# Low parts and gated products on VectorE, nine-step reciprocal roots, and ctx ahead of x in the last part of a SwiGLU layer

## The chip, the core and the metric

The kernel runs on one core of one Trainium2 chip (trn2). The metric is the device time of one execution in microseconds (us), the median of three runs. A core has TensorE (PE in the profile, its weight loads PEld), VectorE (DVE), ScalarE (ACT), GpSimd (POOL), SyncE (SP, which issues the weight DMAs here) and DMA engines.

## What is computed

Two transformer blocks of two layers each, width 1024, 512 tokens of x and, in the second block, 256 tokens of a context ctx. All in fp32. Cut to what matters here:

```
# first block, two layers
h = rms_norm(x, g_norm1[l]) * (1 + sc1) + sh1
u = h @ w_in[l] + b_in[l]                       # latents, stick-breaking q/k/v, gates
x = x + gt1 * (merged @ w_out[l])               # merged: two attentions, gated
h = rms_norm(x, g_norm2[l]) * (1 + sc2) + sh2
up = causal_depthwise_conv(h @ w_up[l], w_conv[l], b_conv[l])
a, v_ff = split(up)
x = x + gt2 * ((silu(a) * v_ff) @ w_down[l])    # silu(a) * v_ff: the gated product
# second block, layer 0: convolution mixer for x and ctx, then
x = x + gf_x * rmsnorm(swiglu(fx, w1, w3, w2), g)
ctx = ctx + gf_c * rmsnorm(swiglu(fc, w1, w3, w2), g)
# layer 1: attention, queries of x, keys and values of x and ctx; then swiglu of x alone
```

mod (sh, sc, gt) comes from products of a silu vector with modulation weights; the second block has one such vector for x and one for ctx.

## The kernel before, in words

Activations lie transposed, 8 tiles of 128 features by 512 tokens. A matmul in fp32 quality is made of three in a faster format: each weight chunk and each activation is split into a high part (rounded, `hi`) and a low part (`lo` = value minus high), and `dense` (L176 to L186) adds hi*hi, hi*lo and lo*hi in PSUM (L184, L185, L186). `dense_tok` (L188 to L194) does the same with the activation as the stationary side.

`weights` (L157 to L168) loads a chunk of 128 x up to 1024 by SP's DMA queue into `raw`, lets ACT round it into `whi` (L165), and subtracts to get `wlo` (L168). The subtraction runs on VectorE, or on POOL for each `lo_pool`-th chunk. `lo_pool` is 2 from the first full-width up of a first-block layer to that layer's end, 1 in the last part of the attention loop (`WO_LATE`), 2 for the output projection of the second half (`LO_O`), and 0 elsewhere. So half of the chunks of a first-block feed-forward stretch have their low part made by POOL.

That stretch (the last third of `first_layer`) has 22 pairs of ups in three parts, FFN_PARTS, with eight downs behind each part. `up` (L731 to L753) multiplies both branches, ACT and VectorE make the three-tap convolution from PSUM (L740, L744, L745), ACT makes Silu (L751), POOL the gated product (L752), and `split` makes the high part on ACT (L282) and the low part on VectorE (L285). A down's result is added to x by VectorE (L778), which also frees the PSUM tile. The first three pairs and the last downs run in two halves of 256 tokens. Between these, side work multiplies modulation weight rows by one vector (layer 0) or two (layer 1) on VectorE (L308, tiles `mjunk`), in program order.

`rstd_psum` (L226 to L244) sums squares by matmuls with a column of 1/1024 (L238), adds epsilon on VectorE (L240), calls `rsqrt` (L197 to L211), and broadcasts the root by transposes (L243). `rsqrt` starts from an integer shift and subtraction (L204, L205), halves (L206), and repeats three steps three times (L208 to L210). `modulate` and `post_norm` use the broadcast: of eight feature tiles VectorE takes five products (L261), POOL three (L259).

In the second block `ffn2` runs a list of steps by part; each step is an up or a down for a group of streams: sx is all of x, sa and sb its halves, st is ctx. At the last part's downs, `ffn_done` is called per stream: post norm and residual, then the pre norm for attention. In `attention_layer`, `PROJ` is the order of projections: (stream, g) with stream 0 = A, 1 = B (halves of x), 2 = ctx, and g = a half of the query heads or None for keys and values. Queries and keys are normed per head (with `rsqrt` again), turned by rope (VectorE L1082, POOL L1084) and transposed by TensorE (L1091). Then come 64 units of scores, with the output projection of the first half of x (w_o) inside the loop; that of the second half follows behind it.

The order within each engine's queue is fixed at build time by a planner that simulates the engines' times and takes instructions in program order where that is free; TensorE, VectorE, ACT and POOL then each run their queue in order, and waits are by semaphores between queues.

Of the kernel before, what the change touches and what calls it, by code (L numbers as in the profile page):

```python
# [81 lines left out]
LO_O = 2  # L82
# [14 lines left out]
class Core:  # L97


    def __init__(self, ctx, tc, a):  # L100
        self.tc, self.nc, self.a = tc, tc.nc, a
        nc = self.nc
        self.const = ctx.enter_context(tc.tile_pool(name="const", reuse_waits="tile", bufs=1))
        self.res = ctx.enter_context(tc.tile_pool(name="res", reuse_waits="tile", bufs=1))
        self.wp = ctx.enter_context(tc.tile_pool(name="wp", reuse_waits="tile", bufs=1))
        self.sm = ctx.enter_context(tc.tile_pool(name="sm", reuse_waits="tile", bufs=4))
        self.ps = None
        c = self.const
# [12 lines left out]
        self.chunks = 0  # L121
        self.lo_pool = 0
# [36 lines left out]
    def weights(self, src, n):  # L159
# [37 lines left out]
    def rsqrt(self, v, n, step=False):  # L197
        nc = self.nc
        y = self.sm.tile([P, 32], F32, tag="rs_y", name="rs_y", bufs=3)
        hv = self.sm.tile([P, 32], F32, tag="rs_h", name="rs_h", bufs=2)  # L200
        b = self.sm.tile([P, 32], F32, tag="rs_b", name="rs_b", bufs=2)
        y, hv, b = y[:, :n], hv[:, :n], b[:, :n]
        t = b.bitcast(I32)
# [21 lines left out]
    def rstd_psum(self, sums):  # L225
# [9 lines left out]
        v = self.sm.tile([P, 4], F32, tag="rs_v", name="rs_v", bufs=2)  # L235
# [4 lines left out]
        nc.vector.tensor_scalar(v[:, :nt], ps[:, :nt], EPS, None, op0=ALU.add)  # L240
        r, last = self.rsqrt(v[:, :nt], nt, True)
# [141 lines left out]
def mla_heads(core, tmp, pool, kp, l, ups, cos, sin, rows):  # L383
# [28 lines left out]
    for w, width in enumerate((256, 128)):  # L412
        nc.vector.tensor_scalar(vv[:, :, w], ss[:, :, w], 1.0 / width, EPS, op0=ALU.mult, op1=ALU.add)
# [56 lines left out]
    vq = sm.tile([P, 16], F32, tag="vq", name="vq", bufs=1)  # L470
    nc.vector.tensor_scalar(vq, ssq, 1.0 / 192, EPS, op0=ALU.mult, op1=ALU.add)
# [26 lines left out]
    vk = sm.tile([P, 16], F32, tag="vk", name="vk", bufs=1)  # L498
    nc.vector.tensor_scalar(vk, ssk.rearrange("p a b -> p (a b)"), 1.0 / 192, EPS, op0=ALU.mult, op1=ALU.add)
    rk = core.rsqrt(vk, 16)  # L500
# [166 lines left out]
def first_layer(core, pool, l, ups, mod, cos, sin, next_mod, early, finish):  # L667
# [58 lines left out]
    with tc.tile_pool(name=f"ff{l}", reuse_waits="tile", bufs=1) as fp:  # L726
        tails = {}

        def up(i, hl, cols):
# [22 lines left out]
            nc.gpsimd.tensor_tensor(av[0], av[0], av[1], op=ALU.mult)  # L752
            core.split(hl[0][:, cols], hl[1][:, cols], av[0])  # L753

        for part, (k0, k1) in enumerate(FFN_PARTS):
# [5 lines left out]
            if part == 0:  # L761
                next_mod(fp)
                core.lo_pool = 2
# [21 lines left out]
        core.lo_pool = 0  # L785
# [54 lines left out]
def ffn2(core, fp, i, bases, parts, nbuf, finish):  # L840
# [3 lines left out]
    for part, (k0, k1, steps) in enumerate(parts):  # L844
        first, last = part == 0, part == len(parts) - 1
        hid = {b.tag: [core.pair(fp, b.n, "hid" + b.tag, nbuf) for _ in range(k0, k1)] for b in bases}
        core.lo_pool = 0
# [35 lines left out]
    core.lo_pool = 0  # L883


def conv_layer(core, X, A, B, T, post, pre, between):
# [4 lines left out]
    with tc.tile_pool(name="cv_c", reuse_waits="tile", bufs=1, side="right") as cp, ExitStack() as es:  # L891
# [92 lines left out]
        core.lo_pool = CONV_LO  # L984
# [28 lines left out]
        core.lo_pool = 0  # L1013
# [29 lines left out]
def attention_layer(core, pool, A, B, T, axial, tables, dense_psum, finish):  # L1043
# [4 lines left out]
    with ExitStack() as es:  # L1048
# [8 lines left out]
        with tc.tile_pool(name="at_t", reuse_waits="tile", bufs=1) as tmp:  # L1057
# [39 lines left out]
            def keys(st, pss):  # L1097
# [5 lines left out]
                nc.vector.tensor_scalar(v, v, 1.0 / 64, EPS, op0=ALU.mult, op1=ALU.add)  # L1103
                rk = core.rsqrt(v, 8)
# [33 lines left out]
            core.lo_pool = PROJ_LO  # L1138
            for st, g in PROJ:
# [6 lines left out]
                if g == 1:  # L1146
                    v = rq[half].rearrange("p a b -> p (a b)")
                    nc.vector.tensor_scalar(v, v, 1.0 / 64, EPS, op0=ALU.mult, op1=ALU.add)
                    nc.vector.tensor_scalar(v, core.rsqrt(v, 32), float(64.0 ** -0.5), None, op0=ALU.mult)
            core.lo_pool = 0  # L1150
# [3 lines left out]
        with tc.tile_pool(name="at_p", reuse_waits="tile", bufs=1) as pp, core.psum_pool("ps_a") as pa:  # L1154
# [69 lines left out]
            for u in range(64 + 4):  # L1224
# [26 lines left out]
        core.lo_pool = 0  # L1251
# [3 lines left out]
def emit(tc, a, out, stop=None):  # L1255
    nc = tc.nc
    with ExitStack() as ctx:
# [147 lines left out]
        with tc.tile_pool(name="y0", reuse_waits="tile", bufs=1) as yp:  # L1405
# [12 lines left out]
            def ffn_done(s):  # L1418
# [9 lines left out]
                     (18, 22, [(up, [sx]), (down, [sa]), (down, [sb]), (up, [st]), (down, [st])]))  # L1428
# [144 lines left out]
```

## Time and profile before

| what | us |
|---|---|
| median of three runs (3200.9, 3206.35, 3206.95) | 3206.35 |
| the profiled execution's own time | 3205.2 |
| its span, first to last instruction | 3203.2 |
| TensorE busy | 3026.3 |
| VectorE busy | 2094.5 |
| ScalarE busy | 1378.0 |
| GpSimd busy | 556.8 |
| mean granted TensorE clock | 0.976 |

A group's row of the profile reads: line, engine, operation, output<-inputs by the program's names, shapes, xcount, then busy us, mean ns of one, and idle time of the engine just before them with what ended it. A timeline's row reads: start, duration, engine, line, operation, and in brackets the wait before it and who ended it. Matmuls are pipelined and their ends modelled.

### The profile page before, as it was taken

How to read it: one execution, taken by the hardware profiler on the slowest of the kernel's cores; microseconds unless marked ns; L12 is line 12 of the kernel's file. 1: busy time of each engine (PE TensorE's matmuls, PEld its weight loads, DVE VectorE, ACT ScalarE, POOL GpSimd, SP SyncE). 2: the span in 40 equal slices, each digit the busy share in tenths (PEclk: the TensorE clock that was granted, in tenths of full speed). 3: DMA queues.
4: the chain of work that ended last, by engine and by line, in shares of the span. 5: the costliest groups of instructions: out<-in, count | busy, mean ns of one | idle time of the engine just before them, and what ended most of it. 6: DMA issues, size and time to landing. Idle time of an engine off the chain costs nothing.

```text
span 3203.2 us, 45064 instructions
## 1 busy us (share of the span) xinstructions
PE 3026.3 (94%) x16916; PEld 2541.2 (79%) x16916; DVE 2094.5 (65%) x3973; ACT 1378.0 (43%) x2521; POOL 556.8 (17%) x508
## 2 busy tenths in 40 slices
PE   6999999999899999999999899999999889999998
PEld 5776888888777697777866688888888667898887
DVE  7654785657643588798898686544549976673336
ACT  4534562335534563224522574221226556553223
POOL 4000223333000213223334120000002311210001
PEclk9999999999999999999999899999999889999999
DMA  6443346554321254554544345234435310243323
GB/s 235 135 147 100 120 164 204 176 203 143 100 66 56 85 193 154 180 193 138 160 140 123 106 145 178 87 118 135 134 101 167 121 35 17 76 144 109 98 98 120
DMA packets 129322, 416.69 MB, mean 130 GB/s; under 512 B 16208, under 2 KB 21840, under 8 KB 129104
## 3 DMA queue, kind: packets, MB, share of 16 engines
q1 hardware_dynamic: 123984, 404.96, 38.8%
q0 software_dynamic: 2048, 4.43, 0.5%
q10 hardware_dynamic: 3072, 4.43, 0.5%
q8 instruction: 133, 2.18, 0.3%
q14 instruction: 85, 0.70, 0.1%
HBM read 402.81 MB, written 2.10 MB: 126 GB/s over the span
## 4 chain that ended last, share of the span: by engine, by line
PE 42%; DVE 7%; ACT 1%; DMA 1%; issue 1%; POOL 0%; ACTq 0%; DVEq 0%; POOLq 0%
PE pa L185 4%; PE pa L184 4%; PE pa L186 4%; PE pv L186 3%; PE pv L184 3%; PE pv L185 3%; PE dn L186 3%; PE dn L184 3%; PE dn L185 3%; PE cv L948 2%; PE yps L1198 2%; DVE wlo L168 1%; DVE hp L261 1%; PE pT L1187 1%; PE sc L1165 1%
## 5 line engine op out<-in xcount | busy, mean ns | idle before, releaser
L165 ACT CAST whi<-raw 128x1024 fp32r<-128x1024 f32 (+4 forms) x622 | 599.3, 967 | 1008.4 <-PE dn L185 296.4
L168 DVE TENSOR_TENSOR wlo<-raw,whi 128x1024 fp32r<-128x1024 f32 (+4 forms) x543 | 620.9, 1145 | 366.0 <-ACT whi L165 357.6
L184 PE MATMUL dn<-hi,whi 128*128 128x256 f32 (+1 forms) x1088 | 361.9, 336 | 19.4 <-DVE x L778 13.5
L185 PE MATMUL dn<-lo,whi 128*128 128x256 f32 (+1 forms) x1088 | 362.6, 335 | 1.6 <-DVE lo L285 1.5
L186 PE MATMUL dn<-hi,wlo 128*128 128x256 f32 (+1 forms) x1088 | 359.7, 334 | 3.3 <-DVE wlo L168 3.1
L184 PE MATMUL up<-hh,whi 128*128 128x512 f32 (+1 forms) x800 | 292.0, 366 | 7.2 <-ACT hh L269 7.2
L185 PE MATMUL up<-hl,whi 128*128 128x512 f32 (+1 forms) x800 | 292.6, 366 | 0.4 <-DVE hl L270 0.4
L186 PE MATMUL up<-hh,wlo 128*128 128x512 f32 (+1 forms) x800 | 291.8, 365 | 0.0
L259 POOL TENSOR_TENSOR hp<-hp,rb 128x256 f32<-128x256 f32 x90 | 76.5, 862 | 1151.0 <-ACT hp L258 1136.6
L168 POOL TENSOR_TENSOR wlo<-raw,whi 128x1024 fp32r<-128x1024 f32 (+1 forms) x79 | 194.1, 2458 | 391.9 <-ACT whi L165 388.7
L308 DVE SCALAR_TENSOR_TENSOR mjunk<-mraw,crow 128x1024 f32<-128x1024 f32 (+1 forms) x176 | 220.5, 1253 | 42.9 <-PE g L185 21.1
L184 PEld LDWEIGHTS dn<-hi,whi 128*128 128x128 f32 x1088 | 205.8, 190 | 47.0 <-issue 14.0
L186 PEld LDWEIGHTS dn<-hi,wlo 128*128 128x128 f32 x1088 | 205.2, 189 | 28.2 <-DVE wlo L168 5.5
L185 PEld LDWEIGHTS dn<-lo,whi 128*128 128x128 f32 x1088 | 206.7, 190 | 25.0 <-DVE lo L285 2.3
L184 PE MATMUL pa<-hh,whi 128*128 128x512 f32 (+1 forms) x496 | 179.8, 362 | 7.1 <-ACT hh L269 6.4
L185 PE MATMUL pa<-hl,whi 128*128 128x512 f32 (+1 forms) x496 | 178.6, 360 | 0.2
L186 PE MATMUL pa<-hh,wlo 128*128 128x512 f32 (+1 forms) x496 | 178.0, 359 | 0.0
L184 PEld LDWEIGHTS up<-hh,whi 128*128 128x128 f32 x800 | 152.3, 191 | 31.6 <-ACT hh L269 7.7
L185 PEld LDWEIGHTS up<-hl,whi 128*128 128x128 f32 x800 | 152.6, 191 | 24.7 <-DVE hl L270 1.0
L186 PEld LDWEIGHTS up<-hh,wlo 128*128 128x128 f32 x800 | 152.4, 191 | 23.6
L860 DVE TENSOR_TENSOR s<-s,pv 128x512 f32<-128x512 f32 (+1 forms) x76 | 40.9, 539 | 196.0 <-PE pv L186 196.0
L186 PE MATMUL pv<-hh,wlo 128*128 128x512 f32 (+1 forms) x432 | 152.6, 353 | 0.7 <-DVE wlo L168 0.7
(471 smaller groups left out, 7349.5 us busy)
## 6 DMA issues: line engine op xcount, KB each, us to landing
raw<-in_w SPq DMA_DIRECT2D x148, 512.0 KB, 3.5
raw<-in_w_up SPq DMA_DIRECT2D x100, 512.0 KB, 3.5
mraw<-in_w_modt SPq DMA_DIRECT2D x96, 512.0 KB, 3.5
mraw<-in_w_adat SPq DMA_DIRECT2D x80, 512.0 KB, 3.4
raw<-in_w_pw SPq DMA_DIRECT2D x56, 512.0 KB, 3.4
raw<-in_w_down SPq DMA_DIRECT2D x48, 448.0 KB, 3.4
raw<-in_w_g SPq DMA_DIRECT2D x32, 512.0 KB, 3.2
raw<-in_w_out SPq DMA_DIRECT2D x32, 512.0 KB, 3.5
```

What stands on the lines that cost most here:

```text
L165: nc.scalar.copy(hi[:, :n], raw[:, :n])
L168: eng.tensor_tensor(lo[:, :n], raw[:, :n], hi[:, :n], op=ALU.subtract)
L184: mm(out, lhsT=hi[:, k, :], rhs=xh[:, cols], start=(k == 0), stop=False)
L185: mm(out, lhsT=hi[:, k, :], rhs=xl[:, cols], start=False, stop=False)
L186: mm(out, lhsT=lo[:, k, :], rhs=xh[:, cols], start=False, stop=(k == n - 1))
L259: nc.gpsimd.tensor_tensor(p, p, rb[1], op=ALU.mult)
L261: nc.vector.scalar_tensor_tensor(p, x, scale, rb[0], op0=ALU.mult, op1=ALU.mult)
L308: behind(nc.vector.scalar_tensor_tensor(junk, raw, 1.0, v, op0=ALU.mult, op1=ALU.mult, accum_out=d[:, f : f + 1]))
L860: nc.vector.tensor_tensor(s, s, pv, op=ALU.mult)
L948: nc.tensor.matmul(ps[32 * g : 32 * g + 32, :], lhsT=wt[:, 8 * g + j, :], rhs=ug[g][:, 4 * j : 4 * j + S], start=(j == 0), stop=(j == 7))
L1165: nc.tensor.matmul(ps[:, b, :384], lhsT=q, rhs=khT[:, hd // 4, ks], start=True, stop=False)
L1198: nc.tensor.matmul(yps[64 * e : 64 * e + 64, :], lhsT=V[j][:, kvh * 64 : (kvh + 1) * 64], rhs=pairs[p][1][e][:, j, :], start=(j == 0), sto ...
```

## The change

All low parts of weights are made on VectorE: `lo_pool`, `PROJ_LO`, `CONV_LO`, `WO_LATE` and `LO_O` go. The gated product of the first block goes from POOL to VectorE. `rsqrt` takes scale, epsilon and a factor in its first instruction and needs nine instructions, with a start and steps of other constants; the instructions that added epsilon and scaled around it go, and two that multiplied behind it become copies. In the last part of the first SwiGLU layer of the second block, up and down of ctx come first, then up of x and the downs of its halves; the keys and values of ctx become the first projection.

```diff
-PROJ = ((0, 0), (0, 1), (0, None), (1, 0), (1, None), (2, None), (1, 1))
-WO_LATE = 3
+PROJ = ((2, None), (0, 0), (0, 1), (0, None), (1, 0), (1, None), (1, 1))
...
         nc.scalar.copy(hi[:, :n], raw[:, :n])
-        self.chunks += 1
-        eng = nc.gpsimd if self.lo_pool and self.chunks % self.lo_pool == 0 else nc.vector
-        eng.tensor_tensor(lo[:, :n], raw[:, :n], hi[:, :n], op=ALU.subtract)
+        nc.vector.tensor_tensor(lo[:, :n], raw[:, :n], hi[:, :n], op=ALU.subtract)
...
-    def rsqrt(self, v, n, step=False):
+    def rsqrt(self, v, n, scale=1.0, factor=1.0, step=False):
...
-        nc.vector.tensor_scalar(t, v.bitcast(I32), 1, None, op0=ALU.logical_shift_right)
-        nc.vector.tensor_scalar(y.bitcast(I32), t, -1, 0x5F3759DF, op0=ALU.mult, op1=ALU.add)
-        nc.vector.tensor_scalar(hv, v, -0.5, None, op0=ALU.mult)
-        for _ in range(3):
-            nc.vector.tensor_tensor(b, y, y, op=ALU.mult)
-            nc.vector.tensor_tensor(b, b, hv, op=ALU.mult)
-            last = nc.vector.scalar_tensor_tensor(y, b, 1.5, y, op0=ALU.add, op1=ALU.mult)
+        k = -0.5 / (3.375 * factor) ** 2
+        nc.vector.tensor_scalar(w, v, scale * k, EPS * k, op0=ALU.mult, op1=ALU.add)
+        nc.vector.tensor_scalar(y.bitcast(I32), w.bitcast(I32), -0.5, float(0x5F375A86 - 2**22 - 2**30),
+                                op0=ALU.mult, op1=ALU.add)
+        nc.vector.tensor_tensor(b, y, y, op=ALU.mult)
+        nc.vector.tensor_tensor(b, b, w, op=ALU.mult)
+        nc.vector.scalar_tensor_tensor(c, b, 5.0 / 3.0, b, op0=ALU.add, op1=ALU.mult)
+        nc.vector.scalar_tensor_tensor(c, c, 1.25, y, op0=ALU.add, op1=ALU.mult)
+        nc.vector.tensor_tensor(b, c, c, op=ALU.mult)
+        nc.vector.tensor_tensor(b, b, w, op=ALU.mult)
+        last = nc.vector.scalar_tensor_tensor(y, b, 2.0 / 3.0, c, op0=ALU.add, op1=ALU.mult)
...
-        nc.vector.tensor_scalar(v[:, :nt], ps[:, :nt], EPS, None, op0=ALU.add)
-        r, last = self.rsqrt(v[:, :nt], nt, True)
+        r, last = self.rsqrt(ps[:, :nt], nt, step=True)
...
-    rq0 = core.rsqrt(vq, 16)
+    rq0 = core.rsqrt(ssq, 16, 1.0 / 192, 192.0 ** -0.5)
     rq = sm.tile([P, 16], F32, tag="rq", name="rq", bufs=1)
-    nc.vector.tensor_scalar(rq, rq0, float(192.0 ** -0.5), None, op0=ALU.mult)
+    nc.vector.tensor_copy(rq, rq0)
...
             nc.scalar.activation(av[0], av[0], AF.Silu)
-            nc.gpsimd.tensor_tensor(av[0], av[0], av[1], op=ALU.mult)
+            nc.vector.tensor_tensor(av[0], av[0], av[1], op=ALU.mult)
...
                 v = ss.rearrange("p a b -> p (a b)")
-                nc.vector.tensor_scalar(v, v, 1.0 / 64, EPS, op0=ALU.mult, op1=ALU.add)
-                rk = core.rsqrt(v, 8)
+                rk = core.rsqrt(v, 8, 1.0 / 64)
...
-                     (18, 22, [(up, [sx]), (down, [sa]), (down, [sb]), (up, [st]), (down, [st])]))
+                     (18, 22, [(up, [st]), (down, [st]), (up, [sx]), (down, [sa]), (down, [sb])]))
```

## Rows read from the trace of the kernel before

**Rows 1.** The page's first part: an engine's busy us, share, instructions.

```profile
PE 3026.3 (94%) x16916; PEld 2541.2 (79%) x16916; DVE 2094.5 (65%) x3973; ACT 1378.0 (43%) x2521; POOL 556.8 (17%) x508
```

**Rows 2.** Busy time by stretch, core 0: layer 0, then layer 1 of the first block.

```profile
core 0: us, PE busy (x) PEld busy (x) DVE busy (x) ACT busy (x) POOL busy (x), PEclk, DMA share, GB/s
485.00:755.00 270.00, 269.53 (x1208) 221.86 (x1206) 156.09 (x222) 92.64 (x117) 84.07 (x42) 1.00 0.55 180
...
1240.00:1500.00 260.00, 247.39 (x1062) 201.13 (x1061) 223.09 (x291) 83.49 (x105) 74.82 (x36) 0.97 0.55 178
```

**Rows 3.** TensorE's waits, whole span: total us, times, longest us.

```profile
PE rb L243 <- DVE rs_y L210: 19.8, 11, 4.1
PE dn L184 <- DVE x L778: 13.5, 5, 6.9
...
PE rb L238 <- DVE acc L221: 12.6, 3, 9.7
```

**Rows 4.** Busy time by stretch: the passage to attention, and just before it.

```profile
2393.00:2593.00 200.00, 167.40 (x971) 143.20 (x971) 182.29 (x436) 116.91 (x216) 63.22 (x65) 0.92 0.42 135
...
2350.00:2393.00 43.00, 43.00 (x205) 36.14 (x204) 13.36 (x16) 11.48 (x16) 0.00 (x0) 1.00 0.22 68
```

**Rows 5.** The page's fifth part: low parts on POOL (busy us, mean ns | idle).

```profile
L168 POOL TENSOR_TENSOR wlo<-raw,whi 128x1024 fp32r<-128x1024 f32 (+1 forms) x79 | 194.1, 2458 | 391.9 <-ACT whi L165 388.7
```

**Rows 6.** Groups of POOL, 1240 to 1500 us.

```profile
L168 POOL TENSOR_TENSOR wlo<-raw,whi 128x1024 fp32r<-128x1024 f32 x18 | 47.2, 2624 | 53.0 <-ACT whi L165 53.0
...
L752 POOL TENSOR_TENSOR up<-up 128x512 f32<-128x512 f32 x14 | 18.1, 1291 | 110.6 <-DVE up L745 92.5 <-ACT up L740 18.1
```

**Rows 7.** Timeline of VectorE, 1274 to 1285 us: start, us, line, operation.

```profile
1275.77 3.27 DVE L308 SCALAR_TENSOR_TENSOR mjunk<-mraw,ccrow 128x1024 f32<-128x1024 f32 x1
```

**Rows 8.** Timeline of POOL, the same stretch; two instructions in one row.

```profile
1274.66 6.58 POOL L168 TENSOR_TENSOR wlo<-raw,whi 128x1024 fp32r<-128x1024 f32 x2 [3.99 <-ACT whi L165]
```

**Rows 9.** Timeline of TensorE, the same stretch; in brackets the wait before.

```profile
1279.85 0.47 PE L184 MATMUL dn<-hi,whi 128*128 128x512 f32 x1 [3.09 <-DVE x L778]
```

**Rows 10.** Groups of VectorE, 1240 to 1500 us, with POOL at work.

```profile
L308 DVE SCALAR_TENSOR_TENSOR mjunk<-mraw,ccrow 128x1024 f32<-128x1024 f32 x46 | 63.4, 1379 | 0.7
L308 DVE SCALAR_TENSOR_TENSOR mjunk<-mraw,crow 128x1024 f32<-128x1024 f32 x45 | 59.8, 1328 | 3.0 <-DMA mraw<-in_w_modt 2.6
L285 DVE TENSOR_TENSOR lo<-up,hi 128x512 fp32r<-128x512 f32 x14 | 28.4, 2030 | 19.2 <-ACT hi L282 19.2
```

**Rows 11.** Groups of VectorE, 2000 to 2400 us, with POOL idle.

```profile
L308 DVE SCALAR_TENSOR_TENSOR mjunk<-mraw,crow 128x1024 f32<-128x1024 f32 x40 | 48.8, 1219 | 3.2 <-DMA mraw<-in_w_modt 3.2
...
L168 DVE TENSOR_TENSOR wlo<-raw,whi 128x1024 fp32r<-128x1024 f32 x33 | 40.4, 1224 | 32.7 <-ACT whi L165 32.4
...
L285 DVE TENSOR_TENSOR lo<-s,hi 128x512 fp32r<-128x512 f32 x18 | 12.4, 691 | 9.8 <-ACT hi L282 9.6
...
L308 DVE SCALAR_TENSOR_TENSOR mjunk<-mraw,ccrow 128x1024 f32<-128x1024 f32 x8 | 9.8, 1221 | 0.1
```

**Rows 12.** Timeline of VectorE: a root at the second half's output projection.

```profile
2778.47 0.16 DVE L240 TENSOR_SCALAR rs_v<-rb 128x2 f32<-128x2 f32 x1 [0.94 <-PE rb L238]
...
2780.25 2.25 DVE L208 TENSOR_TENSOR rs_b<-rs_y 128x2 f32<-128x2 f32 x1
```

**Rows 13.** Timeline of TensorE behind it: two waits.

```profile
2796.96 0.58 PE L186 MATMUL wo<-hh,wlo 128*128 128x256 f32 x1 [3.10 <-DVE wlo L168]
...
2811.03 0.58 PE L184 MATMUL pa<-hh,whi 128*128 128x256 f32 x1 [1.66 <-ACT hh L269]
```

**Rows 14.** Groups of VectorE in the passage to attention, 2393 to 2593 us.

```profile
L168 DVE TENSOR_TENSOR wlo<-raw,whi 128x1024 fp32r<-128x1024 f32 x39 | 50.2, 1288 | 4.6 <-ACT whi L165 4.5
...
L221 DVE TENSOR_TENSOR acc<-acc,sqx 128x256 f32<-128x256 f32 x36 | 17.4, 491 | 0.1
...
L168 DVE TENSOR_TENSOR wlo<-raw,whi 128x512 fp32r<-128x512 f32 x21 | 14.9, 721 | 2.5 <-ACT whi L165 2.4
...
L270 DVE SCALAR_TENSOR_TENSOR ctx_hl<-hp,mod,ctx_hl 128x256 fp32r<-128x256 f32 x8 | 4.4, 593 | 0.0
```

**Rows 15.** TensorE's waits in the same passage.

```profile
PE pj L192 <- DVE rp L1082: 4.8, 1, 4.8
```

More of the change, by code (lines that the diff above doesn't have):

```diff
@@ L81 @@
 YB = 1
-LO_O = 2
 GATE_TAGS = ("hp",) * 5 + ("rb",) * 3 + ("acc",) * 2 + ("sqx",) * 4
@@ L120, in __init__ @@
         self.side = iter(())
-        self.chunks = 0
-        self.lo_pool = 0
     def issue_behind(self, ins, others):
@@ L194, in dense_tok @@
         mm(out, lhsT=xl[:, cols], rhs=wh, start=False, stop=last)
-    def rsqrt(self, v, n, step=False):
+    def rsqrt(self, v, n, scale=1.0, factor=1.0, step=False):
         nc = self.nc
+        w = self.sm.tile([P, 32], F32, tag="rs_w", name="rs_w", bufs=2)
         y = self.sm.tile([P, 32], F32, tag="rs_y", name="rs_y", bufs=3)
-        hv = self.sm.tile([P, 32], F32, tag="rs_h", name="rs_h", bufs=2)
         b = self.sm.tile([P, 32], F32, tag="rs_b", name="rs_b", bufs=2)
-        y, hv, b = y[:, :n], hv[:, :n], b[:, :n]
-        t = b.bitcast(I32)
-        nc.vector.tensor_scalar(t, v.bitcast(I32), 1, None, op0=ALU.logical_shift_right)
-        nc.vector.tensor_scalar(y.bitcast(I32), t, -1, 0x5F3759DF, op0=ALU.mult, op1=ALU.add)
-        nc.vector.tensor_scalar(hv, v, -0.5, None, op0=ALU.mult)
-        for _ in range(3):
-            nc.vector.tensor_tensor(b, y, y, op=ALU.mult)
-            nc.vector.tensor_tensor(b, b, hv, op=ALU.mult)
-            last = nc.vector.scalar_tensor_tensor(y, b, 1.5, y, op0=ALU.add, op1=ALU.mult)
+        c = self.sm.tile([P, 32], F32, tag="rs_c", name="rs_c", bufs=2)
+        w, y, b, c = w[:, :n], y[:, :n], b[:, :n], c[:, :n]
+        k = -0.5 / (3.375 * factor) ** 2
[9 more added lines that the diff above has]
+        last = nc.vector.scalar_tensor_tensor(y, b, 2.0 / 3.0, c, op0=ALU.add, op1=ALU.mult)
         return (y, last) if step else y
@@ L234, in rstd_psum @@
             ps, pb = self.mm_psum("ms"), self.at_psum("rb")
-        v = self.sm.tile([P, 4], F32, tag="rs_v", name="rs_v", bufs=2)
         for t in range(nt):
@@ L412, in mla_heads @@
     for w, width in enumerate((256, 128)):
-        nc.vector.tensor_scalar(vv[:, :, w], ss[:, :, w], 1.0 / width, EPS, op0=ALU.mult, op1=ALU.add)
+        nc.vector.tensor_scalar(vv[:, :, w], ss[:, :, w], 1.0 / width, None, op0=ALU.mult)
     r = core.rsqrt(v, 8)
@@ L469, in mla_heads @@
         nc.vector.tensor_copy(qrT[:, :, sl], tp.rearrange("p (a b) -> p a b", b=P))
-    vq = sm.tile([P, 16], F32, tag="vq", name="vq", bufs=1)
-    nc.vector.tensor_scalar(vq, ssq, 1.0 / 192, EPS, op0=ALU.mult, op1=ALU.add)
-    rq0 = core.rsqrt(vq, 16)
+    rq0 = core.rsqrt(ssq, 16, 1.0 / 192, 192.0 ** -0.5)
     rq = sm.tile([P, 16], F32, tag="rq", name="rq", bufs=1)
-    nc.vector.tensor_scalar(rq, rq0, float(192.0 ** -0.5), None, op0=ALU.mult)
+    nc.vector.tensor_copy(rq, rq0)
     wkv = core.chunk(a["w_ukv"][l])
@@ L497, in mla_heads @@
         kt.append(kn)
-    vk = sm.tile([P, 16], F32, tag="vk", name="vk", bufs=1)
-    nc.vector.tensor_scalar(vk, ssk.rearrange("p a b -> p (a b)"), 1.0 / 192, EPS, op0=ALU.mult, op1=ALU.add)
-    rk = core.rsqrt(vk, 16)
+    rk = core.rsqrt(ssk.rearrange("p a b -> p (a b)"), 16, 1.0 / 192)
     for t in range(TOK):
@@ L762, in first_layer @@
                 next_mod(fp)
-                core.lo_pool = 2
             for i in range(k0 + apart, k1):
@@ L784, in first_layer @@
                     finish(cols, sums)
-        core.lo_pool = 0
 class Base:
@@ L882, in ffn2 @@
             yield
-    core.lo_pool = 0
 def conv_layer(core, X, A, B, T, post, pre, between):
@@ L983, in conv_layer @@
         us = []
-        core.lo_pool = CONV_LO
         core.side = taps_dve(us)
@@ L1012, in conv_layer @@
         es.close()
-        core.lo_pool = 0
         pre(T)
@@ L1136, in queries @@
                                qT[half][2 * g + hb][:, :, t * P : t * P + P], hb == 1)
-            core.lo_pool = PROJ_LO
             for st, g in PROJ:
@@ L1147, in attention_layer @@
                     v = rq[half].rearrange("p a b -> p (a b)")
-                    nc.vector.tensor_scalar(v, v, 1.0 / 64, EPS, op0=ALU.mult, op1=ALU.add)
-                    nc.vector.tensor_scalar(v, core.rsqrt(v, 32), float(64.0 ** -0.5), None, op0=ALU.mult)
-            core.lo_pool = 0
+                    nc.vector.tensor_copy(v, core.rsqrt(v, 32, 1.0 / 64, 64.0 ** -0.5))
         dense_psum.close()
@@ L1250, in attention_layer @@
             B.squares(core, B.yv(m), m)
-        core.lo_pool = 0
         finish(B)
```

6 lines of the change are left out of this document (removed).

## The prediction

> **What bounds the kernel now.** I read the page first, then the busy time by stretch, then TensorE's waits, then the stretches where it waits. TensorE is busy for 94% of the span [rows 1], so nothing off its path is worth anything where it is full, and the whole 177 us that it is idle is the most that better feeding could give. The up and down stretch of the first block's layer 0 shows a full stage: TensorE 269.53 of 270 us, VectorE 156 [rows 2]. The same stretch of layer 1 isn't full: TensorE 247 of 260 at a mean granted clock of 0.97, VectorE 223 [rows 2]. The difference is the side work: two modulation rows per weight row there, one in layer 0. TensorE's longest waits by cause are the broadcast that waits for a reciprocal root (19.8 us in 11 waits), down matmuls that wait until VectorE has emptied their PSUM (13.5), and sums that wait for VectorE's additions (12.6) [rows 3]. The worst long stretch is the passage from the second block's first SwiGLU layer to attention: in 200 us TensorE is busy for 167 at a clock of 0.92, while VectorE is busy for 182; just before it, in the last ups of x, TensorE is full and VectorE works 13 of 43 us [rows 4]. So there VectorE is the bound, and some of its work could be done earlier.
>
> **Low parts and gated product.** By the code, 35 low parts of each first-block layer and nine of the second block are on POOL: the 79 of the page [rows 5]. With them go 50 gated products, of 512 and 256 columns. POOL takes 2.6 us for a low part and 1.3 for a product [rows 6]; the question is what VectorE pays. Alone, VectorE takes about 1.22 us for 1024 elements from two SBUF tensors and 0.69 for 512 [rows 11]. So 22 low parts and 14 products of the stretch of layer 1 add 22 x 1.22 + 14 x 0.69 = 36 us to VectorE's 223 of 260. But it already pays for POOL's work: a modulation row that begins at 1275.77 takes 3.27 us [rows 7], and it ends 1.1 us, its own working time, after POOL's first low part (two of them fill 1274.66 to 1281.24, half of that is 3.29 [rows 8]). It stood still until POOL was done. Behind it stands the emptying of a PSUM tile, for which TensorE waits 3.09 us [rows 9]. Over this stretch the split's low part takes 2030 ns against 691 alone, the two kinds of modulation row 1379 and 1328 against 1221 and 1219 [rows 10, 11]: 14 x 1.34 + 46 x 0.16 + 45 x 0.11 = 31 us that go with POOL's work. Net, VectorE gets 5 us more in 260. That is within its 37 idle us, but in order, so it can help or hurt: bounds are minus 20 us (260 less 247 that TensorE is idle [rows 2], and some of the slow clock behind its waits) and plus 10 (the 5 us twice, with the clock lost behind). The product adds a wait to VectorE, for Silu on ACT, with the low parts and the emptying of PSUM queued behind it; Silu reads the first branch's tile, which is done while TensorE still multiplies the second (24 x 0.22 us), so the wait should be nothing. I take minus 3: the net is near nothing, and the chain up, Silu, product, hi, lo gets 0.6 us shorter at each pair (1.29 to 0.69), which counts at the layer's end.
> In layer 0 the same addition lies beside a full TensorE (156 plus some 36 of 270): 0; without that cover it would cost what exceeds VectorE's 114 idle us, which is nothing. The five low parts inside attention take at most 5 x 1.23 = 6 us if each stands in front of a maximum that TensorE needs; I take 0, since POOL's broadcast of the totals is freed of a predecessor of 2.5 us [rows 5] as well. At the output projection of the second half, a step of the root is held from 0.16 to 2.25 us by POOL [rows 12], and TensorE waits 3.10 us for a low part and 1.66 for the first h [rows 13]. Four low parts more cost 4 x 1.23 = 4.9 us on VectorE; three such holds give back 3 x 2.1 = 6.3. Bounds plus 5 and minus 5, taken: minus 2.
> A rule speaks against this: the Trainium skill (Perfetto Trace Analysis, Optimizing Scalar/DVE Operations) says that with VectorE saturated some work may be moved to ScalarE or even GpSimd; that would make this part a loss, which is the second rival. The same place warns that the two share an SBUF read port, so that this need not help, and with the warning the trace agrees [rows 7 to 11].
>
> **Shorter roots.** The code goes from 13 VectorE instructions a root (addition of epsilon, shift, subtraction, halving, three times three) to nine. Dependent steps are 0.18 us apart (2778.47 to 2780.25 is ten steps) [rows 12], so an exposed root gets 3 to 4 steps, some 0.6 us, shorter; halving lay beside another step. There are 31 roots of norms and 11 of heads and latents by the code. Exposed are those before which TensorE waits: the 11 waits of [rows 3] less three in the attention passage, counted below, plus the start and three or four hidden behind "sum" and h waits: 13 x 0.6 = 8 us. Lower bound 4 (only the eight seen), upper 14 (where a step stands behind other work in VectorE's queue, each step saved saves an instruction of 0.4 to 1.2 us, too). The multiplication after the roots of q becomes a copy of the same size: 0.
>
> **ctx ahead of x.** Up and down of ctx move before the ups of x, with their 8 + 8 weight DMAs, ACT's rounding and VectorE's low parts; keys of ctx become the first projection. SP's weight queue keeps its order of need, and no queue gets more to do. What moves off VectorE's crowded stretch: 8 low parts at 0.72 and 8 at 1.29 (16.1 us), a third of the 36 additions (5.9), ctx's own low halves (4.4) [rows 14], and, alike for ctx as for each half of x, its additions, products and splits (some 14, estimated from five to eight each at 0.4 to 0.55) and a third of the roots' steps (5): 45 us of 182. It goes under the ups of x, where VectorE is idle for 30 of 43 us [rows 4], and under its own 288 half-width matmuls. These, at half of 0.223 us (270 us by 1208 matmuls [rows 2]), are 32 us of TensorE, 35 with the two sums. So 165 of the 200 us stay, with 137 us of VectorE work, 129 with shorter roots (8 off: 12 roots by four steps of 0.16 us). At its present share (182 of 200) that is 142: minus 23. Not all of it comes: today A's normalisation is covered by the down of B and all of ctx (46 us); afterwards by the down of B (96 x 0.112 = 11 us) and the keys of ctx (48 x 0.223 = 11, and transposes 2). From the root to the first h used takes 32.6 us in the like place (2778.47 to 2811.03) [rows 12, 13], so TensorE waits some 9 us for h at A's queries, of which VectorE uses about half. I take minus 18. Bounds: minus 36 (VectorE never idle) and plus 5 (nothing gained, half of the wait paid). The wait of 4.8 us before the keys of ctx [rows 15] goes; next late is the tail, POOL's rope and the transposes behind it, which don't change.
>
> **The sum.** Minus 5, minus 8, minus 18: minus 31 us from the profiled execution's 3205.2 (span 3203.2 and 2.0 around it; the median of the runs is 1.15 higher): 3174 us.
>
> **Rivals.** First: the order pays nothing, since A's normalisation, in a crowded VectorE queue, comes 25 us late instead of 9. For it speaks that VectorE is busy for 91% of that stretch; against it that 45 us of work leave the queue. Time: 3205 - 13 = 3192, chance 0.14. Second, on the slow side: VectorE becomes the bound in layer 1 of the first block, because what was stretched there waits for something else than POOL. Then 35 low parts at 1.22 and 25 products at 0.4 to 0.69 add 57 us where 37 of 260 are idle; it decides once more than 26 us of them (the gain of roots and order) aren't hidden. All hidden that can be: 3205 + 20 - 26 = 3199; half of the idle usable: 3218; none: 3236. Against it speaks that the stretched piece begins its work where POOL's ends [rows 7 to 9]: 0.07. Third: the planner that orders each engine's queue by simulated times puts ctx's work back where it was, and roots are hidden by their neighbours; only 0 to 8 us remain: 3200 to 3206, chance 0.07. The forecast has 0.72, its own range 3158 to 3192.
>
> **The numbers.** The range reaches from minus 55 (the order at minus 30, roots 12, low parts 13) to minus 6: 3150 to 3199; the second rival and most of the third lie outside. About 0.2%, 6.4 us, is what a measurement of this kernel can tell from no change. Faster takes the forecast, 0.12 of the first rival and 0.01 of the third: 0.85. Same takes the rest of these two, 0.08; slower the second rival, 0.07.
>
> **What would show it.** Right: no POOL work between 1240 and 1500, the split's low part near 0.69 us, modulation rows near 1.22; nine steps a root, 1.5 us; the stretch from the downs of x to the first scores some 20 us shorter than 165, without a wait for ctx. Wrong: TensorE's waits for emptied PSUM in layer 1 above 20 us, or a wait for A's h above 20 us behind the keys of ctx.

## The result, and the profile after

| | us |
|---|---|
| after, median of four runs (3149.32 to 3153.33) | 3152.18 |
| before, median of four runs (3200.9 to 3206.95) | 3205.99 |
| ratio, 95% interval | 0.9834 (0.9817 to 0.9851) |
| profiled span, before and after | 3203.2, 3147.6 |

The kernel is 54 us faster; the forecast was 31 with a range of 6 to 55. The page's first part of after, answering to [rows 1]: TensorE's busy time falls by 21 us though it issues the same 16916 matmuls, at a mean granted clock of 0.980 (0.976 before), so part of the gain goes with the clock; VectorE is busy for 16 us more, POOL for 244 less.

```profile
PE 3005.1 (95%) x16916; PEld 2543.3 (81%) x16916; DVE 2110.8 (67%) x3936; ACT 1372.7 (44%) x2521; POOL 312.7 (10%) x379
```

Busy time by stretch of after (columns as in [rows 2, 4]): layer 0, layer 1 with the attention end before it, the ups of x, the crowded part of the passage.

```profile
485.00:755.00 270.00, 269.12 (x1229) 224.34 (x1228) 194.27 (x268) 95.89 (x122) 0.00 (x0) 1.00 0.57 181
1200.00:1500.00 300.00, 299.30 (x1354) 248.11 (x1352) 273.55 (x416) 111.07 (x152) 2.92 (x3) 1.00 0.55 178
2350.00:2393.00 43.00, 43.00 (x210) 36.13 (x209) 29.91 (x65) 20.57 (x40) 7.00 (x9) 1.00 0.25 75
2393.00:2545.00 152.00, 130.02 (x672) 109.60 (x670) 136.16 (x306) 88.14 (x159) 59.53 (x56) 0.90 0.42 137
```

Layer 1 is now as full as layer 0, at full clock, although VectorE is busy for 91% of it (86% before). The crowded part of the passage, from the downs of x to the first scores, is shorter, but its shares have hardly changed: VectorE 90% (91% in the 200 us of [rows 4]), TensorE 86% (84%), clock 0.90 (0.92).

Groups of VectorE in layer 1 of after, 1230 to 1475 us, beside [rows 10]: all three stand at the lone durations of [rows 11], the time that such an instruction takes while POOL is idle.

```profile
L303 DVE SCALAR_TENSOR_TENSOR mjunk<-mraw,crow 128x1024 f32<-128x1024 f32 x46 | 56.1, 1219 | 1.6 <-DMA mraw<-in_w_modt 1.5
L303 DVE SCALAR_TENSOR_TENSOR mjunk<-mraw,ccrow 128x1024 f32<-128x1024 f32 x46 | 56.1, 1219 | 0.2
...
L280 DVE TENSOR_TENSOR lo<-up,hi 128x512 fp32r<-128x512 f32 x15 | 10.3, 685 | 2.7 <-ACT hi L277 2.7
```

TensorE's waits of after over the whole span, beside [rows 3]: the 11 waits for a finished root (19.8 us) are 3, and those on x (13.5 us) are almost gone; those for sums have grown from 12.6 to 21.9.

```profile
PE rb L234 <- DVE acc L218: 21.9, 5, 8.8
...
PE rb L238 <- DVE rs_y L207: 8.1, 3, 4.3
...
PE dn L176 <- DVE x L768: 0.9, 2, 0.4
```

Where the time went is read by following the same matmuls in both traces (the n-th into a tile of a name). Each entry is how much less time the stage took than before, in us; plus is longer. "lo", "prod", "roots" and "order" are single parts of the change on the kernel before, from the first experiments below.

| stage (time in the trace of before) | after | lo | prod | roots | order |
|---|---|---|---|---|---|
| to layer 1's ups, 0 to 1240 | -3.1 | -1.7 | -1.7 | +2.1 | -4.0 |
| layer 1's ups and downs, 1240 to 1565 | -27.3 | -21.2 | -10.4 | +0.6 | +0.2 |
| convolution layer, 1565 to 1990 | -6.8 | -1.9 | +0.7 | -7.4 | -0.1 |
| SwiGLU and passage, 1990 to 2599 | -10.3 | -1.0 | -1.6 | -8.0 | -4.4 |
| attention, 2599 to 2775 | -0.2 | -0.2 | +1.4 | 0.0 | +1.4 |
| output projection, finish, 2775 to 2849 | -4.0 | -2.6 | -0.2 | -4.3 | -0.4 |
| to the end | -3.7 | +0.8 | 0.0 | -0.8 | -1.7 |

Each column comes from one profiled execution. Differences of up to 4 us in a stage also arise where the code is the same (0 to 1240 of the column "order"). Between medians taken on different chips some 4 us are open, too: those of the kernel before lie between 3202.0 and 3206.0.

### The profile page after: what moved, and what is told of

Its sections match the earlier page's. It is cut to its first block, busy times and chain, and to the rows that moved or that the text cites. A ratio compares the mean times of both kernels' runs of the same rounds, so it can differ in the third digit from the quotient of the medians.

```text
span 3147.6 us, 44851 instructions
## 1 busy us (share of the span) xinstructions
PE 3005.1 (95%) x16916; PEld 2543.3 (81%) x16916; DVE 2110.8 (67%) x3936; ACT 1372.7 (44%) x2521; POOL 312.7 (10%) x379
## 3 DMA queue, kind: packets, MB, share of 16 engines
q8 instruction: 133, 2.18, 0.3%
## 5 line engine op out<-in xcount | busy, mean ns | idle before, releaser
L160 DVE TENSOR_TENSOR wlo<-raw,whi 128x1024 fp32r<-128x1024 f32 (+4 forms) x622 | 712.0, 1147 | 402.1 <-ACT whi L159 393.5
L176 PE MATMUL pv<-hh,whi 128*128 128x512 f32 (+1 forms) x432 | 151.9, 352 | 0.0
```

Source lines behind the costliest of these rows:

```text
L160: nc.vector.tensor_tensor(lo[:, :n], raw[:, :n], hi[:, :n], op=ALU.subtract)
L176: mm(out, lhsT=hi[:, k, :], rhs=xh[:, cols], start=(k == 0), stop=False)
```

## The experiments

Three theories for layer 1. T1: while POOL reads two SBUF tensors, VectorE's instructions with SBUF operands stand still, and at the starts of the downs one stands ahead of the addition to x. T2: a low part from POOL is late by itself. T3: the product on POOL made the downs late. Each run is compared with the kernel before on the same chip.

**Each part alone, on the kernel before.**

```diff
# b_lo
-        eng = nc.gpsimd if self.lo_pool and self.chunks % self.lo_pool == 0 else nc.vector
+        eng = nc.vector
# b_prod
-            nc.gpsimd.tensor_tensor(av[0], av[0], av[1], op=ALU.mult)
+            nc.vector.tensor_tensor(av[0], av[0], av[1], op=ALU.mult)
# b_root: rsqrt and its callers as in the change
# b_order: PROJ and the last part's steps as in the change
```

> The kernel before with one edit: all low parts of weights on VectorE, the gated product still on POOL. T1 (POOL's two-tensor work keeps VectorE's instructions with two SBUF inputs standing until POOL ends, and the removal of that is the gain of layer 1): 22 of the 36 POOL instructions of layer 1's stretch and some 58 of 75 us of POOL's work there go, so most of the gain: minus 18 to minus 25 us, nearly all of it between the first full-width up of layer 1 and its last down; the split's low part in layer 1 falls from 2030 ns to below 1000, and rows of modulation to about 1250 or less. T2 (a low part from POOL is only late, 2.6 us instead of 1.2, and TensorE waits for it): also minus 18 to minus 25, but before has TensorE waits on wlo from POOL in layer 1, and rows of modulation stay at 1330 to 1380 ns. T3 (the longer chain over POOL's product of 1.29 us made the downs late): within 5 us of before. As the prediction had it (low parts nearly neutral): minus 2 to minus 5.

> The kernel before with one edit: the gated product on VectorE, half of the low parts of weights still on POOL. T1: 14 of 36 POOL instructions and some 17 of 75 us of POOL's work in layer 1 go, and VectorE gets 14 x 0.69 = 10 us more: between plus 3 and minus 8 us, the split's low part in layer 1 still above 1500 ns. T2: 0 (plus or minus 3). T3: minus 15 to minus 25 us, and TensorE's waits on x at the downs of layer 1 are gone.

> The kernel before with one edit: reciprocal roots in nine instructions. The prediction has minus 8 (minus 4 to minus 14); the two traces, compared at the same places of TensorE's queue, put minus 12 to minus 14 beside norms outside layer 1 and the passage. If the saving were only the exposed roots' own steps: minus 8. If whole slots behind other VectorE work are saved as well, in the passage too: minus 14 to minus 20. If neighbours hide them: 0 to minus 4.

> The kernel before with one edit: up and down of ctx first in the last part of the second block's first SwiGLU layer, and keys and values of ctx as the first projection. The prediction has minus 18 (plus 5 to minus 36); the two traces show minus 10 over the passage with all parts of the change together, roots among them. If the wait for A's normalisation takes back half of the gain: minus 6 to minus 10, with a gap of 8 to 10 us on TensorE behind the keys of ctx. If roots made part of those 10: minus 3 to minus 7. First rival of the prediction (order pays nothing): plus or minus 2.

| run | median us | ratio to before, interval | us |
|---|---|---|---|
| b_lo | 3176.44 | 0.9917 (0.9903 to 0.9930) | -27 |
| b_prod | 3193.03 | 0.9968 (0.9956 to 0.9979) | -10 |
| b_root | 3182.90 | 0.9937 (0.9924 to 0.9951) | -20 |
| b_order | 3200.37 | 0.9989 (0.9980 to 0.9997) | -4 |

The us are the ratio less one, by 3203.28, the median of before in these runs. The four add up to 61, against 54 for the whole: in layer 1 low parts and product together gain 27.3, less than 21.2 and 10.4, because they empty the same waits (on x 13.1 us before, 1.0 in b_lo, 6.8 in b_prod). Low parts are the largest part, and the group rows of b_lo, 1240 to 1480 us, tell T1 from T2. Rows of modulation, which no low part feeds, are back at 1.22 us; T2 had them stay at 1.33 to 1.38. T2 also needs waits of TensorE on low parts from POOL in layer 1 of before, and there are none (the list stands in the part on the prediction). POOL's product in its turn now takes 1802 ns where it took 1291 [rows 6].

```profile
L308 DVE SCALAR_TENSOR_TENSOR mjunk<-mraw,crow 128x1024 f32<-128x1024 f32 x44 | 53.6, 1219 | 1.1 <-DMA mraw<-in_w_modt 1.0
L308 DVE SCALAR_TENSOR_TENSOR mjunk<-mraw,ccrow 128x1024 f32<-128x1024 f32 x44 | 53.6, 1217 | 0.3
```

```profile
L752 POOL TENSOR_TENSOR up<-up 128x512 f32<-128x512 f32 x14 | 25.2, 1802 | 216.8 <-DVE up L745 151.1 <-ACT whi L165 38.0 <-ACT up L740 27.7
```

For b_prod no theory was right: 10 us is 2 more than T1 gave at most, more than T2's 3, and too little for T3, which had the waits on x gone. T1 missed a sign as well: the split's low part was to stay above 1500 ns and takes 913. TensorE's waits in layer 1 (1230 to 1560 us) keep the longest of them; POOL's low parts are still there, and the rows of modulation that ccrow feeds take 1590 ns.

```profile
PE dn L184 <- DVE x L778: 6.8, 2, 6.4
```

**The disputed mechanism by itself, on the kernel after.** POOL gets work that nobody uses, in the first block's feed-forward stretches, at every second chunk.

```diff
# a_readpool, in weights(), behind VectorE's subtraction
+        if self.extra is not None and self.chunks % 2 == 0:
+            for c in (slice(0, n // 2), slice(n // 2, n)):
+                nc.gpsimd.tensor_tensor(self.extra[:, : n // 2], raw[:, c], hi[:, c], op=ALU.subtract)
# a_copypool: in its place
+                nc.gpsimd.tensor_copy(self.extra[:, : n // 2], hi[:, c])
```

> The kernel after, with POOL work added that nobody uses: in the feed-forward stretches of the first block, for every second weight chunk, POOL subtracts hi from raw in two halves into a tile of its own, beside VectorE's subtraction that makes the low part. VectorE's work, and what TensorE waits for, stay the same. T1 (POOL's reading of two SBUF tensors holds VectorE's instructions with two SBUF inputs): 14 to 30 us slower than after, 3166 to 3182, nearly all in layer 1, where the mean of the split's low part rises above 850 ns from 691 and rows of modulation above 1260 ns from 1219, and TensorE's waits on x at the downs come back. T2 (a low part from POOL was late) and T3 (the product's chain): within 5 us of after, 3147 to 3157, since low parts and products still come from VectorE.

> The kernel after, with POOL copies added that nobody uses, of hi alone, in two halves, at the same places and of the same number as the subtractions of the run beside it. If only POOL instructions that read two SBUF tensors hold VectorE: within 4 us of after (3148 to 3157), rows of modulation and split at their lone durations (1219 and 691 ns). If any reading by POOL does: 10 to 25 us slower than after, rows above 1260 ns.

a_readpool took 3188.87 us (ratio 0.9955, 0.9941 to 0.9969): 37 us slower than after, more than T1's 14 to 30, and far from the 5 of T2 and T3. VectorE's order in layer 1 is the same as after's but for six short differences, and layer 1 lost 30 us by the same matmuls (another 9 in the profile lie ahead of it). TensorE's busy time and clock are those of before again, with POOL 85 us busy and VectorE 251 (223 before):

```profile
1240.00:1500.00 260.00, 248.59 (x1075) 202.93 (x1074) 251.09 (x324) 81.85 (x103) 84.64 (x46) 0.97 0.54 178
```

The timelines of POOL, VectorE and TensorE at the first downs show how. POOL runs four subtractions without a pause from 1280.10 to 1288.01. Rows of modulation that begin ahead of it take 1.2 us, those inside it 2.18 and 2.31; the addition to x at 1283.26 stands behind the first of these, and TensorE waits 2.10 us for it, then 3.51 for a low part.

```profile
1280.10 7.91 POOL L166 TENSOR_TENSOR extra<-raw,whi 128x512 f32<-128x512 f32 x4 [15.28 <-ACT whi L161]
```

```profile
1278.61 1.23 DVE L309 SCALAR_TENSOR_TENSOR mjunk<-mraw,ccrow 128x1024 f32<-128x1024 f32 x1
...
1281.15 2.18 DVE L309 SCALAR_TENSOR_TENSOR mjunk<-mraw,ccrow 128x1024 f32<-128x1024 f32 x1
...
1283.26 1.40 DVE L775 SCALAR_TENSOR_TENSOR x<-dn,mod,x 128x512 f32<-128x512 f32 x2
1284.58 2.31 DVE L309 SCALAR_TENSOR_TENSOR mjunk<-mraw,crow 128x1024 f32<-128x1024 f32 x1
```

```profile
1284.15 0.47 PE L182 MATMUL dn<-hi,whi 128*128 128x512 f32 x1 [2.10 <-DVE x L775]
...
1289.15 0.80 PE L184 MATMUL dn<-hi,wlo 128*128 128x512 f32 x1 [3.51 <-DVE wlo L162]
```

The expectation that the split's low part would be held was wrong (715 ns): it hardly runs beside POOL any more. Held are rows of modulation (1366 and 1423 ns) and weights' low parts (1513), which read two SBUF tensors. VectorE's instructions with an operand in PSUM keep their length: the addition to x, 748 ns in after, and the taps of the convolution (739 and 741 ns, 745 and 747 in after).

```profile
L775 DVE SCALAR_TENSOR_TENSOR x<-dn,mod,x 128x512 f32<-128x512 f32 x16 | 11.7, 743 | 2.6 <-PE dn L184 2.6
```

One rival lies in the run itself: POOL's reading also keeps `raw` occupied, and loads of weights waited 12.5 us for it, in 11 waits. But TensorE waits for a high part 0.3 us in layer 1, as in after, so these loads weren't late.

a_copypool took 3156.94 us (0.9854, 0.9840 to 0.9868): 5 us more than after, 2 of them in layer 1; the intervals overlap. Rows stand at 1236 and 1226 ns, low parts of weights at 1325 instead of 1200. So a copy, which reads one SBUF tensor, holds VectorE as well, but costs little. It lies between the two expectations, much nearer the first. POOL is also busy for less time with the copies (53 of the 260 us against 85), so how much of the difference is the second operand, and how much the shorter work, stays open.

**What the order is worth, and what bounds the passage.** Four kernels from after: the old order; POOL's two-tensor work of rope and stacked heads (tiles `stk`, high and low part side by side) on VectorE; VectorE's copies of turned heads (transposed by TensorE into PSUM) on ScalarE; a third order.

```diff
# a_oldorder: PROJ and the last part's steps as before
# v_rope: lines 1069, 1070, 1103, 1117
-                nc.gpsimd.tensor_tensor(...)
+                nc.vector.tensor_tensor(...)
# v_cast
-                (nc.scalar.copy if act else nc.vector.tensor_copy)(dst, tp.rearrange("p (a b) -> p a b", b=P))
+                nc.scalar.copy(dst, tp.rearrange("p (a b) -> p a b", b=P))
# v_mid
+PROJ = ((0, 0), (0, 1), (2, None), (0, None), (1, 0), (1, None), (1, 1))
+                     (18, 22, [(up, [st]), (up, [sx]), (down, [sa]), (down, [st]), (down, [sb])]))
```

> The kernel after, with the old order of the last SwiGLU part and of the projections: what the order is worth beside the other two parts. Alone it gave 2.9 us (0.1% to 0.2%). If VectorE's load is what it relieves, roots relieve the same, and it is worth 0 to 4 here: 3151 to 3157. The prediction's minus 18 would make it 3170. If it now costs (the sum of the three other parts alone, minus 27, 10 and 20, is 57 of the 54 found): 3147 to 3151.

> The kernel after, with POOL's remaining two-tensor work in attention's passage (rope's two combinations and the low parts of the stacked heads, 30 instructions of some 39 us) on VectorE. T1 carried further: VectorE pays some 30 x 0.6 = 18 us, and what its two-tensor instructions stood behind POOL goes; the waits of TensorE's transposes on POOL (5.8 us) go: 3 to 10 us faster than after, 3142 to 3149. If VectorE is the bound of this passage and wasn't held there: 3 to 12 us slower, 3155 to 3164.

> The kernel after, with the 14 copies of turned heads that VectorE makes (0.68 us each, 9.5 us in all) on ScalarE, which has 62 us free in the crowded stretch of the passage (busy 86.6 of 149.1 us, VectorE 135.7). If VectorE's load is what bounds that stretch: 9.5 us less of it at its share of 91%, minus 5 to minus 10 us, 3142 to 3147. If the chain over rope, stacked heads, transposes and copies bounds it, whoever copies: within 2 us of after, 3150 to 3154. If ScalarE's queue (rounding of weights, squares) is late then: plus 2 to plus 8.

> The kernel after, with another order: in the last part ups of ctx, ups of x, downs of A, downs of ctx, downs of B; then queries of A, keys of ctx, keys of A, B's. The downs of ctx and of B then cover A's norm. If the wait for A's norm (5.5 and 1.7 us) is what kept the order's gain small: minus 4 to minus 7 against after, 3145 to 3148. If VectorE's load in the crowded stretch is (ctx's norm and additions are back in it): plus 0 to plus 5, 3152 to 3157.

| run | median us | ratio to before, interval | last part to first scores, us |
|---|---|---|---|
| before | | | 241.2 |
| b_order | 3200.37 | 0.9989 (0.9980 to 0.9997) | 236.7 |
| b_root | 3182.90 | 0.9937 (0.9924 to 0.9951) | 233.4 |
| a_oldorder | 3153.85 | 0.9844 (0.9831 to 0.9858) | 235.2 |
| after | 3152.18 | 0.9834 (0.9817 to 0.9851) | 231.1 |
| v_cast | 3148.88 | 0.9827 (0.9812 to 0.9842) | 231.0 |
| v_rope | 3156.22 | 0.9854 (0.9836 to 0.9871) | 234.8 |
| v_mid | 3168.45 | 0.9889 (0.9872 to 0.9905) | 247.4 |

The order is worth 4 us in the profiles, alone and with the rest, and by the times 4 alone (1 to 6) and 2 with the rest, where the intervals overlap. The passage by stretches: before, b_order, a_oldorder, after and v_cast, each from the first down of its crowded part to the first scores. With the new order, up and down of ctx lie ahead of it.

```profile
2389.80:2587.40 197.60, 167.99 (x989) 144.11 (x988) 181.90 (x435) 114.74 (x213) 63.22 (x65) 0.93 0.43 138
```

```profile
2424.10:2579.00 154.90, 131.16 (x682) 107.96 (x680) 140.20 (x340) 86.19 (x157) 57.79 (x56) 0.90 0.41 135
```

```profile
2352.90:2544.60 191.70, 168.21 (x990) 143.86 (x988) 170.16 (x391) 114.15 (x213) 64.43 (x65) 0.94 0.43 142
```

```profile
2390.80:2539.90 149.10, 129.61 (x682) 109.47 (x680) 135.70 (x304) 86.58 (x157) 59.53 (x56) 0.90 0.43 140
```

```profile
2393.70:2542.80 149.10, 128.13 (x682) 107.73 (x680) 130.33 (x290) 93.11 (x171) 60.17 (x56) 0.91 0.42 140
```

v_cast has 5.4 us less VectorE time in this stretch (of the 9.5 taken out, the rest went into longer rows), and it stays at 149.1 us, with VectorE's share down from 91% to 87%. That speaks against VectorE's load as what sets its length; it is one profiled execution, and the 5 us expected otherwise are little more than the 4 by which a stage varies. Its median is the lowest of all runs, 3 us under after between the two expectations, but not told apart from after. What is left there is single waits of TensorE, the longest for A's sum and h behind the keys of ctx, and for the transposes' stacked heads at the end (after, 2300 to 2600 us):

```profile
PE rb L234 <- DVE acc L218: 5.5, 1, 5.5
PE qT L1076 <- POOL stk L1117: 3.4, 2, 2.5
PE sc L1146 <- ACT ctx_hl L1163: 3.3, 5, 2.7
PE qT L1076 <- ACT stk L1102: 3.1, 1, 3.1
PE qT L1076 <- POOL stk L1103: 2.4, 2, 1.5
PE pj L184 <- ACT hh L264: 1.7, 1, 1.7
```

v_rope removes POOL from these and lost 4 us, with overlapping intervals, where T1 had 3 to 10 gained: the wait moves to ACT's stacked heads (6.2 us) and VectorE's. Yet VectorE had been held here, too: it runs 38 instructions more, 30 of them 16.5 us by their rows, and its busy time over the whole span grows by 4.9 us only (2110.8 to 2115.7). What it got back isn't what TensorE waited for. v_mid, meant to cover A's sum, lost 16, and neither of its expectations had that: sums wait for additions 10.2 us in two places and for the steps of a root another 4.8.

```profile
PE rb L234 <- DVE acc L218: 10.2, 2, 8.8
...
PE rb L234 <- DVE rs_c L203: 4.8, 1, 4.8
```

**The lesson carried to other places, on the kernel after.** v_tiles takes POOL out of the norms (`POOL_TILES = ()`): 90 products and 30 additions to x and ctx. The expectation below has POOL's products read one SBUF and one PSUM operand; by the code that is wrong. POOL multiplies by a copy of the broadcast in SBUF, so both its operands lie there; it is VectorE's products (L256 in after) that read the broadcast in PSUM. v_start takes POOL out of the start, where both operands are in SBUF, too (the products and the low parts, lines 1295 and 1323, on VectorE).

> The kernel after, with all products of norms on VectorE, none on POOL: 90 products of POOL at 0.9 us, 24 and 6 additions of 1.07 and 0.85 go, and VectorE gets 90 at 0.47 and 30 at 0.42. If POOL's reading of one SBUF and one PSUM operand held VectorE too, it costs nothing or gains up to 10 us (3142 to 3152). If it doesn't hold VectorE and shared the work truly: 5 to 15 us slower, 3157 to 3167, since each of 31 norms has a chain of three products more (1.4 us) ahead of the last h tiles, where TensorE waits in eleven of them and VectorE is the bound of the passage.

> The kernel after, with POOL's 16 two-tensor instructions of the start (8 products of the first norm, 8 low parts of the first h; 25.2 us of POOL between 20 and 60 us) on VectorE, which is busy for 38.35 of these 40 us. T1 as a rule for other places: VectorE pays 16 x 0.69 = 11 us and gets back what it stood still behind POOL: additions of one column at 1.2 instead of 0.15 us, low parts of weights at 2.1 instead of 1.1, some 13 us. So 0 to 6 us faster, 3146 to 3152, and no instruction of one column above 0.3 us there. If VectorE wasn't held but merely slow at such sizes, it pays the 11 us: 5 to 11 us slower, 3157 to 3163.

v_tiles took 3167.06 us (0.9883, 0.9868 to 0.9898), 15 slower. The time is the one expected if POOL doesn't hold VectorE, and the rows say that it does: additions to x on VectorE take 703 ns in after and 415 in v_tiles, while VectorE's products, with their operand in PSUM, stay at 472 and 473. VectorE's busy time rises by 9.4 us only (2110.8 to 2120.2) for 120 instructions more.

```profile
L819 DVE TENSOR_TENSOR x<-x,hp 128x256 f32<-128x256 f32 x40 | 26.7, 703 | 0.0
```

```profile
L819 DVE TENSOR_TENSOR x<-x,hp 128x256 f32<-128x256 f32 x64 | 23.8, 415 | 0.0
```

So a hold by itself doesn't decide: here it costs less than the longer chain of a norm on one engine. That this chain is what costs the 15 us is argued, not shown; TensorE's waits for a finished root grow from 8.1 to 11.5 us and those for sums from 21.9 to 24.2.

v_start took 3156.86 (0.9853, 0.9838 to 0.9868), 5 slower than after, with overlapping intervals, where 0 to 6 faster was expected. In its own place it did what was expected: after, then v_start, 20 to 60 us.

```profile
20.00:60.00 40.00, 23.94 (x101) 21.74 (x102) 38.35 (x63) 14.48 (x22) 25.24 (x15) 0.84 0.59 202
```

```profile
20.00:60.00 40.00, 33.35 (x133) 29.36 (x134) 34.12 (x82) 16.73 (x24) 0.00 (x0) 0.99 0.67 242
```

VectorE does 19 instructions more in 4 us less, its one-column additions fall to 155 ns each from 513, and TensorE is busy for 9 us more. But 1.8 us of that is left at 413 us. From there to the end v_start loses 10 to after, 3 in layer 1's attention and 4 in the passage, whose code it doesn't touch; VectorE's order there differs from after's in 42 places, since the planner arranges the whole queue anew. That this order is what costs the 4 us wasn't tried.

## Why the prediction was right, and where it was wrong

**Direction and range: right**, the time near the range's low end. That the sum came into the range is in part luck: of the three terms two gave more than forecast (44 us together, as single parts) and one less (14), and the low end of the range was added up from an order of 30, roots of 12 and low parts of 13, none of which came. Of the signs, those for layer 1 came (no POOL work from 1230 to 1475, rows at 1.22 us, the split's low part at 0.69); the crowded part is 16 us under 165, not 20.

**Low parts and product, minus 5 forecast, minus 37 as two single parts, 27 of the whole in layer 1.** The mechanism stood in the prediction (rows stretched until POOL ends, behind them the emptied PSUM). The step that failed was to set the price by VectorE's net load: 5 us more work in 37 idle us, hence minus 3. It was the place that paid. The load was off, too: for the same matmuls, the stage of 1240 to 1565 us, VectorE's busy time fell by 4 us though it runs 44 instructions more; its share rose because the stage got shorter. So more than the 31 us counted went with POOL. Before, then after:

```profile
1240.07:1565.22 325.15, 305.22 (x1465) 254.25 (x1464) 277.45 (x382) 119.36 (x168) 104.43 (x73) 0.97 0.52 167
```

```profile
1237.00:1534.72 297.72, 296.57 (x1466) 251.09 (x1465) 273.06 (x426) 116.22 (x165) 5.29 (x6) 1.00 0.57 182
```

The bound of minus 20 was too tight as well. TensorE's idle time falls from 19.9 to 1.2 us, and its busy time for the same work by 8.7 us, at a granted clock of 1.00 instead of 0.97: 27.4 together. The prediction's window ended at 1500, ahead of the last downs. TensorE's waits in layer 1 of before, through these (1230 to 1570 us):

```profile
PE dn L184 <- DVE x L778: 13.1, 4, 6.9
PE dn L184 <- ACT hi L282: 3.1, 2, 1.7
PE dn L185 <- DVE lo L285: 1.5, 1, 1.5
PE dn L186 <- DVE wlo L168: 1.2, 2, 0.6
PE pg L184 <- ACT whi L165: 0.7, 1, 0.7
PE pg L186 <- DVE wlo L168: 0.3, 1, 0.3
```

In after, from 1230 to 1535 us, it is 0.4 us on x and 0.3 on a weight's high part. The Trainium skill (Perfetto Trace Analysis, Optimizing Scalar/DVE Operations) says that moving work from a saturated VectorE even to GpSimd may make sense; in layer 1 that would have been wrong, VectorE being busy for 86% of it. The same place warns that the two share an SBUF read port, so that this might not help; with that a_readpool agrees (37 us slower), though no trace shows the port itself. Layer 0 at 0 was right (269.53 and 269.12 of 270). The output projection's minus 2 was right (minus 2.6).

**Roots, minus 8 forecast, minus 20.** The saving of one root was right: alone in VectorE's queue it takes 1.7 us in after (2436.23 to 2437.96), 2.3 before (1795.67 to 1798.00). Mis-sized was the number of places where it counts. TensorE's waits for a finished root fell by 11.7 us in after and by 13.7 in b_root (19.8 to 6.1), more than the 8. The passage, where the crowded part's VectorE work fell from 181.9 to 169.9 us and 7.8 us of time with it, was booked with the order. The stage of the convolution layer gave 7.4, of which 1.9 are idle time of TensorE and the rest is busy time, at a granted clock of 0.96 instead of 0.95; how much of that rest is the roots' stays open, since b_lo, which has the same code there, is 5 us less busy in that stage, too.

**Order, minus 18 forecast, minus 4.** The term stood for the passage, and the passage did get 10 us shorter (241.2 to 231.1). But some 8 of the 18 were the shorter roots (129 us of work instead of 137), which belong to the other term: alone they shorten the passage by 7.8. The rest is read from b_order. VectorE's work in the crowded part fell from 181.9 to 140.2 us, 42 of the 45 forecast, and that part takes 154.9 us; by the prediction's own step (137 us at a share of 0.91, and 5 for A's wait) it would be 156. What the step had wrong lies around it: up and down of ctx with the ups of x take 81.8 us, where 35 and 43.6 were set, so 3 us more; and of the old passage not 165 but 163 us were left, its crowded part being 197.6 long. That the length came out by VectorE's share doesn't make the share a bound, as v_cast warns. The wait for A was priced well: 9 us forecast, 7.2 found in after.

**Rivals.** The first, the order pays nothing, was nearly so, by another way than A's norm 25 us late (7.2 us in after). The second, VectorE as the bound of layer 1, is excluded by after's 299.30 of 300. The third is excluded by the 20 us of the roots.

## What to carry to other kernels

Work given to GpSimd isn't free because GpSimd is idle: while it reads SBUF, VectorE's instructions with two SBUF operands can stand. So look at where VectorE's rows are longer than their lone duration and who waits behind those rows, not at the sum of busy time, which counts a held instruction as work. Taking work off GpSimd pays only where somebody waits behind the hold: it gave 27 us in layer 1, nothing clear in the attention passage and at the start, and cost 15 in the norms. Price a stall by the waits and the lost clock of its whole stage, through its last instruction. A busy share of 91% isn't a proof of a bound: take some work off that engine and see whether the stretch gets shorter.

## What the runs showed of the hardware that wasn't expected

The hold takes small instructions too: with POOL's subtractions halved in size, a row of 1.22 us took 2.2 to 2.3, and at the start a one-column addition of 0.155 us took 1.23. It seems to go both ways: POOL's product took 1802 ns in b_lo, 1291 before. It spares VectorE's instructions with an operand in PSUM: additions to x took 743 ns beside POOL's subtractions and 748 without, the norms' products 472 and 473 with and without POOL. POOL copies (one SBUF operand, 47 in layer 1) raised the rows by 7 to 17 ns only, weights' low parts by 125.
